# State tiles of the sample recurrences in halves, with each half's load queued behind an earlier half's store

## The chip, the cores and the metric

The kernel runs on one core of one Trainium2 chip. The metric is the device time of one execution in microseconds (us), as a median over runs. Below, TensorE is PE (its weight loads PEld), VectorE DVE, ScalarE ACT, GpSimd POOL; SP is SyncE, which here only issues DMAs, one after the other.

## What is computed

One step of a hybrid decoder layer for a prompt (512 tokens) and for 8 samples of 8 tokens each, which share the weights. The change is in the two recurrences of the samples. Each sample carries a state from HBM into the step and back to HBM:

```python
# SSD: h (16 heads, 64, 128 states) per sample
y_inter = jnp.einsum('btgn,bgjpn->btgjp', cc, h) * jnp.exp(cum)[..., None]
h_new = h * jnp.exp(cum[:, -1])[..., None, None] + jnp.einsum('bsgj,bsgjp,bsgn->bgjpn', to_end, xc, bc)
# mLSTM: c (4 heads, 128, 256) per sample, with n as a 257th column
num = jnp.einsum('btsh,bshv->bthv', s, vc) + s_inter[..., None] * jnp.einsum('bthd,bhdv->bthv', qc, c_st)
c_new = scale[..., None, None] * c_st + jnp.einsum('bsh,bshd,bshv->bhdv', w_end, kc, vc)
```

So every state is read once by a matmul that gives a part of the output, is scaled, has a product added, and is stored. The outputs include both new states of all 8 samples in float32.

## The kernel before

One program does the whole layer. Its long part is the projections: `gemm` (L201 to L203) and the token-major `gemm_tok` (L772 to L774, and L764 and L765 for the samples) multiply weights of [128, 128] blocks with activations of 256 or 320 columns; each product takes three matmuls, since weights and activations are split into a high and a low half. `split_w` loads a weight unit of 512 KB into `raw` on SP's queue (L176), casts it on ACT (L181, `whi`), subtracts on DVE (L188, `wlo`) or, for the other half of the columns, on ACT and by an adding DMA from POOL (L185, L186). `raw` has two buffers, `whi` and `wlo` three each.

The order of the instructions of each engine in this part of the program is set before the run, by a scheduler that estimates the times of the whole program. Each engine then works through its list in order: an instruction whose data is not there holds up everything behind it on the same engine. That holds for PE's matmuls and for SP's DMAs. The recurrences are not a phase of their own: the scheduler mixes them into the projections, the SSD part into the stretch from about 110 to 220 us, the mLSTM part into that from about 265 to 390 us.

**SSD samples** (L651 to L737). The pool `ssds` has a tag `t4` of three buffers of [128, 1024] float32. `xdts` and `xes` (inputs of the recurrence, made at L661 and L667) are the first two tiles in it, and the states `h0` the next eight, one for each sample. The profile calls an `h0` tile `h`. A loop of four steps (`b`) takes two samples at a time (`hb`): two loads of 512 KB (L711), then four matmuls `ps_hs` (L715), one for each pair of group `g` and sample `hb`. Each of these has only 32 output rows and writes its own quarter of the PSUM tile's partitions, `q = 32 * (2 * g + hb)`. Then, for each sample, POOL scales the whole state (L722), two matmuls `ps_hu` give the update (L725), DVE adds them half by half (L726), and one store sends the state out (L728). `stacks` (L637 to L649) prepares the operands of the `ps_hu` matmuls.

**mLSTM samples** (L899 to L937). The pool `mls` has a tag `t4` of three buffers of [128, 4, 258] float32 for the states `c0` (the profile: `c`). Here the samples come one at a time: a load of 516 KB (L909), four matmuls `ps_nh` (L911), one for each head `h`, each with 32 output rows in its own quarter, then four matmuls `ps_cu` (L918), each followed by a DVE instruction that scales and adds (L919), and one store (L921).

A float32 matmul is two matmul instructions in the trace, so four such matmuls are shown there as x8.

A buffer is free for the next load once the store of the state that was in it has landed; SP waits for that at the head of its queue, and what stands behind it there waits too, the weight loads of L176 among them.

Of the kernel before, what the change touches and what calls it, by code (L numbers as in the profile page):

```python
# [1 line left out]

# [9 lines left out]
F32 = mybir.dt.float32  # L12
# [3 lines left out]
ALU = mybir.AluOpType  # L16
# [100 lines left out]
def build(nc, tc, ctx, I, O):  # L117
# [24 lines left out]
    def BP(name="b"):  # L142
        return pb.tile([P, 512], F32, name=name, tag="b")
# [490 lines left out]
    ssd_prompt(1)  # L634


    def stacks(pool, a, b, hb, nb=1):  # L637

        r, o = slice(32 * hb, 32 * hb + 32), slice(32 - 32 * hb, 64 - 32 * hb)
        l = slice(64, 96)  # L640
        sa_ = pool.tile([96, a.shape[-1]], F32R, name="sta", tag="sta", bufs=nb)
        sb_ = pool.tile([96, b.shape[-1]], F32R, name="stb", tag="stb", bufs=nb)
# [12 lines left out]
    xes = sd.tile([TS, 16, 64], F32, name="xes", tag="t4", bufs=3)  # L655
    btk = sd.tile([TS, 2, P], F32, name="btk")
    for g in range(2):
        ps = BP("ps_xts")
        for j in range(4):
            TE.transpose(ps[:TS, j * P:(j + 1) * P], xs[:, g * 4 + j, TP:T], ident)  # L660
        V.tensor_tensor(xdts[:, 8 * g:8 * g + 8, :], ps[:TS, :].rearrange("p (h k) -> p h k", h=8),  # L661
                        CT[:TS, 4, 32 + 8 * g:40 + 8 * g].unsqueeze(2).to_broadcast([TS, 8, 64]), op=ALU.mult)
# [16 lines left out]
    for g in range(2):  # L679
        psb = BP("ps_ls")  # L680
        pb3 = psb.rearrange("p (h t) -> p h t", h=8)
        for h in range(8):
            mm(psb[:, h * TS:(h + 1) * TS], sel[:80, 8 * g + h:8 * g + h + 1].to_broadcast([80, P]), cumst[:, TP:T],
               start=h == 0, stop=h == 7, skip_group_check=True)
        A.activation(decs[:, 8 * g:8 * g + 8, :], pb3[:, :, 7:TS:8], AF.Exp)
        lm = sd.tile([TS, 8, TS], F32, name="lms", tag="ts", bufs=1)
        V.tensor_tensor(lm, pb3[:TS], CT[:TS, 4, 8 * g:8 * g + 8].unsqueeze(2).to_broadcast([TS, 8, TS]), op=ALU.subtract)
        G.tensor_tensor(lm, lm, masks8, op=ALU.add)
        A.activation(lm, lm, AF.Exp)
        pcb = BP("ps_cbs")  # L690
        mm(pcb[:TS, :TS], bc[:, g, TP:T], bc[:, 2 + g, TP:T], start=True, stop=True)
        V.tensor_tensor(lm, lm, pcb[:TS, :TS].unsqueeze(1).to_broadcast([TS, 8, TS]), op=ALU.mult)
        for h in range(8):
            k, j = h % 2, (8 * g + h) // 2
            mm(psi[64 * k:64 * k + 64, j * TS:(j + 1) * TS], xdts[:, 8 * g + h, :], lm[:, h, :], start=True, stop=True,
               skip_group_check=True)
    yds = sd.tile([P, 8, TS], F32, name="yds", tag="ts", bufs=1)
    G.tensor_tensor(yds, xs[:, :, TP:T], PAR("dskip").unsqueeze(2).to_broadcast([P, 8, TS]), op=ALU.mult)
# [8 lines left out]
    hbs = [stacks(sd, btk.rearrange("p g k -> p (g k)"), xes.rearrange("p h k -> p (h k)"), hb, 2) for hb in range(2)]  # L707
    for b in range(4):
        hns = [sd.tile([P, 16, 64], F32, name="h0", tag="t4", bufs=3) for _ in range(2)]
        for hb in range(2):  # L710
            S.dma_start(hns[hb], I["h0"][4 * hb + b])  # L711
        for g in range(2):
            for hb in (1, 0):
                q = 32 * (2 * g + hb)
                mm(psh[q:q + 32, :], cpad[:, g, 4 * hb + b, :],  # L715
                   hns[hb][:, 8 * g:8 * g + 8, :].rearrange("p h k -> p (h k)"),
                   start=b == 0, stop=b == 3, skip_group_check=True)
        for hb in range(2):
            bb, hn, (bst, xst) = 4 * hb + b, hns[hb], hbs[hb]
            bm = sd.tile([96, 256], F32R, name="bm", tag="bm", bufs=1)  # L720
            A.activation(bm, bst.bitcast(F32), AF.Copy, scale=C32("bmask")[:96, b:b + 1])
            G.tensor_tensor(hn, hn, decs[:, :, bb:bb + 1].to_broadcast([P, 16, 64]), op=ALU.mult)  # L722
            for g in range(2):
                ps = BP("ps_hu")
                mm(ps, bm[:, g * P:(g + 1) * P], xst[:, g * 512:(g + 1) * 512], start=True, stop=True)  # L725
                V.tensor_tensor(hn[:, 8 * g:8 * g + 8, :], hn[:, 8 * g:8 * g + 8, :],  # L726
                                ps.rearrange("p (h k) -> p h k", h=8), op=ALU.add)
            S.dma_start(O["ssms"][bb], hn.rearrange("p h k -> p (h k)"))  # L728
# [168 lines left out]
    V.tensor_tensor(kws, psk[:TS, :].rearrange("p (h k) -> p h k", h=4),  # L897
                    wendm[:TS, 4, :].unsqueeze(2).to_broadcast([TS, 4, P]), op=ALU.mult)
    for hb in range(2):  # L899
        r = slice(32 * hb, 32 * hb + 32)  # L900
        kst, vst = stacks(ms, kws.rearrange("p h k -> p (h k)"), vts.rearrange("p h k -> p (h k)"), hb)
        psn = BP("ps_nh")
        for h in range(4):
            mm(psn[32 * h:32 * h + 32, 0:257], ds_[r, h, r], vt[4][r, h, 0:257], start=True, stop=False,
               tile_position=(32 * hb, 32 * h), skip_group_check=True)
        for b in range(4):
            bb = 4 * hb + b
            c0 = ms.tile([P, 4, 258], F32, name="c0", tag="t4", bufs=3)
            S.dma_start(c0, I["c0"][bb])  # L909
            for h in range(4):  # L910
                mm(psn[32 * h:32 * h + 32, 0:257], qpad[:, h, bb, :], c0[:, h, 0:257], start=False, stop=b == 3,  # L911
                   skip_group_check=True)
            km = ms.tile([96, 512], F32R, name="km", tag="km", bufs=1)
            A.activation(km, kst.bitcast(F32), AF.Copy, scale=C32("bmask")[:96, b:b + 1])
            cn = c0
            for h in range(4):
                ps = BP("ps_cu")
                mm(ps[:, 0:258], km[:, h * P:(h + 1) * P], vst[:, h * 258:(h + 1) * 258], start=True, stop=True)  # L918
                V.scalar_tensor_tensor(cn[:, h, :], c0[:, h, :], es[:, h, 8 * bb + 7:8 * bb + 8], ps[:, 0:258],  # L919
                                       op0=ALU.mult, op1=ALU.add)  # L920
            S.dma_start(O["cs"][bb], cn)  # L921
# [1490 lines left out]
```

## Time and profile before

| | us |
|---|---|
| time, median of 3 runs (1120.54 to 1121.95) | 1121.05 |
| the profiled execution's own time | 1117.7 |
| its span, first to last instruction | 1115.9 |
| PE busy, share of the span | 1095.6, 98% |
| DVE busy, share | 771.4, 69% |
| ACT busy, share | 609.8, 55% |
| POOL busy, share | 223.5, 20% |
| share of PE in the chain that ended last | 81% |
| DMA queue of SP, share of 16 engines' span | 38.7% |

PE is busy nearly all the time, so a microsecond of work more or less on PE moves the end by about as much, unless it falls into a wait. Where PE's busy time is below the length of a stretch, it waited for something; the view of the waits names what. The profile also gives the clock that PE was granted, as a share of full speed: the mean over the span is 0.996.

### The profile page before, as it was taken

The page shows a single profiled execution, that of the slowest core. Times are in us where ns is not written, and L with a number is a line of the kernel's source. Part 1 is how long each engine was busy: PE and PEld are TensorE (multiplying, and loading weights), DVE is VectorE, ACT ScalarE, POOL GpSimd, SP SyncE. Part 2 cuts the span into 40 slices and gives each one's busy share as a digit, 9 for nine tenths or more (in the row PEclk, how much of TensorE's full clock was granted, in tenths as well). Part 3 has the DMA queues.
Part 4 walks back from the last instruction along what each step waited for, and adds up shares of the span by engine and source line. Part 5 has one row for each costly group of instructions (what it writes and reads, how often), then busy time and mean ns, then how long its engine had stood idle before and what let it go on. Part 6 is the DMA issues. An engine that isn't in the chain of part 4 may idle for free.

```text
span 1115.9 us, 21276 instructions
## 1 busy us (share of the span) xinstructions
PE 1095.6 (98%) x8355; PEld 1043.4 (94%) x8355; DVE 771.4 (69%) x1521; ACT 609.8 (55%) x1130; POOL 223.5 (20%) x309
## 2 busy tenths in 40 slices
PE   9999999899999999999999999999999999999997
PEld 8999889798998999999988889999999999999997
DVE  6796875447786685568745455675578878887655
ACT  6877534246464365566534545644465556556654
POOL 1333544313113021110144401100000210020000
PEclk9999999999999999999999999999999999999999
DMA  6685565536464437973487755742552873397432
GB/s 210 159 165 130 132 180 144 172 71 163 128 204 111 118 101 260 294 279 96 151 268 263 254 204 163 229 158 88 169 157 82 188 170 88 83 234 219 103 138 85
DMA packets 60584, 184.44 MB, mean 165 GB/s; under 512 B 6684, under 2 KB 10908, under 8 KB 59972
## 3 DMA queue, kind: packets, MB, share of 16 engines
q1 hardware_dynamic: 44324, 142.19, 38.7%
q0 software_dynamic: 15872, 40.38, 17.5%
q8 instruction: 65, 1.06, 0.4%
q10 hardware_dynamic: 288, 0.52, 0.1%
q14 instruction: 35, 0.29, 0.1%
HBM read 153.75 MB, written 29.30 MB: 164 GB/s over the span
## 4 chain that ended last, share of the span: by engine, by line
PE 81%; DVE 6%; DMA 6%; ACT 5%; issue 2%; SPq 0%; DVEq 0%; ACTq 0%; POOLq 0%
PE ps_in L201 5%; PE ps_in L203 5%; PE ps_in L202 5%; PE ps_g L1725 3%; PE ps_g L1726 3%; PE ps_g L1727 3%; PE ps_u L1726 2%; PE ps_u L1725 2%; PE ps_u L1727 2%; PE ps_o L201 2%; PE ps_o L203 2%; PE ps_o L202 2%; PE ps_dn L201 2%; PE ps_dn L203 2%; PE ps_dn L1932 2%; PE ps_dn L202 2%
## 5 line engine op out<-in xcount | busy, mean ns | idle before, releaser
L201 PE MATMUL ps_in<-uh,whi 128*128 128x320 f32 (+1 forms) x544 | 165.9, 305 | 0.0
L203 PE MATMUL ps_in<-uh,wlo 128*128 128x320 f32 (+1 forms) x544 | 163.3, 301 | 0.1
L202 PE MATMUL ps_in<-ul,whi 128*128 128x320 f32 (+1 forms) x544 | 162.7, 299 | 0.0
L181 ACT CAST whi<-raw 128x1024 fp32r<-128x1024 f32 (+1 forms) x102 | 102.8, 1011 | 80.6 <-PE ps_in L202 19.5
L188 DVE TENSOR_TENSOR wlo<-raw,whi 128x512 fp32r<-128x512 f32 (+1 forms) x94 | 87.9, 935 | 62.4 <-ACT whi L181 61.8
L201 PEld LDWEIGHTS ps_in<-uh,whi 128*128 128x128 f32 x544 | 103.6, 190 | 2.6 <-issue 1.2
L203 PEld LDWEIGHTS ps_in<-uh,wlo 128*128 128x128 f32 x544 | 103.4, 190 | 2.0 <-issue 1.3
L202 PEld LDWEIGHTS ps_in<-ul,whi 128*128 128x128 f32 x544 | 103.6, 190 | 0.7
L186 POOL DMA_DIRECT2D wlo<-win x32 | 28.3, 886 | 94.5 <-ACT wlo L185 84.0
L1725 PE MATMUL ps_g<-b,whi 128*128 128x288 f32 x144 | 42.7, 297 | 1.2 <-ACT cc L1793 1.0
L1725 PE MATMUL ps_u<-b,whi 128*128 128x288 f32 x144 | 42.8, 298 | 0.0
L1726 PE MATMUL ps_u<-b,whi 128*128 128x288 f32 x144 | 42.5, 295 | 0.0
L1726 PE MATMUL ps_g<-b,whi 128*128 128x288 f32 x144 | 42.5, 295 | 0.0
L201 PE MATMUL ps_xo<-qh,whi 128*128 128x288 f32 x128 | 37.8, 300 | 1.0 <-ACT f_xo L1407 1.0
L201 PE MATMUL ps_o<-mixm_h,whi 128*128 128x256 f32 (+1 forms) x128 | 38.0, 297 | 0.3 <-ACT whi L181 0.3
L201 PE MATMUL ps_xq<-u2h,whi 128*128 128x320 f32 (+1 forms) x128 | 38.2, 303 | 0.0
L774 PE MATMUL ps_v<-wlo,uh 128*128 128x256 f32 x128 | 37.0, 293 | 1.1 <-DMA wlo<-wv 1.1
L202 PE MATMUL ps_xq<-u2l,whi 128*128 128x320 f32 (+1 forms) x128 | 38.0, 298 | 0.0
L203 PE MATMUL ps_xq<-u2h,wlo 128*128 128x320 f32 (+1 forms) x128 | 37.9, 297 | 0.0
L202 PE MATMUL ps_o<-mixm_l,whi 128*128 128x256 f32 (+1 forms) x128 | 37.9, 297 | 0.0
L203 PE MATMUL ps_xo<-qh,wlo 128*128 128x288 f32 x128 | 37.7, 296 | 0.0
L202 PE MATMUL ps_xo<-ql,whi 128*128 128x288 f32 x128 | 37.6, 295 | 0.0
(777 smaller groups left out, 3913.8 us busy)
## 6 DMA issues: line engine op xcount, KB each, us to landing
raw<-win SPq DMA_DIRECT2D x35, 512.0 KB, 3.8
raw<-wout SPq DMA_DIRECT2D x17, 512.0 KB, 4.2
kva<-kc SPq DMA_DIRECT2D x16, 512.0 KB, 6.5
kva<-vc SPq DMA_DIRECT2D x16, 512.0 KB, 6.4
raw<-wxq SPq DMA_DIRECT2D x13, 512.0 KB, 3.8
raw<-wgate SPq DMA_DIRECT2D x13, 512.0 KB, 5.3
raw<-wup SPq DMA_DIRECT2D x13, 512.0 KB, 3.5
wlo<-win POOLq DMA_DIRECT2D x24, 256.0 KB, 5.6
```

Source lines behind the costliest of these rows:

```text
L181: A.copy(hi[:, :n], raw[:, :n])
L186: G.dma_start(lo[:, a:b], src[:, a:b], accum_op=ALU.add)
L188: e.tensor_tensor(lo[:, a:b], raw[:, a:b], hi[:, a:b].bitcast(F32), op=ALU.subtract)
L201: mm(ps, wh, ah, start=i == 0, stop=False)
L202: mm(ps, wh, al, start=False, stop=False)
L203: m = mm(ps, wl, ah, start=False, stop=i == len(tiles) - 1)
L774: m = mm(o, ah, lo[:, j:j + 256], start=False, stop=k == KT - 1, skip_group_check=True)
L1725: mm(ps, wh, b[0][:, k, :], start=start and k == 0, stop=False, skip_group_check=True)
L1726: mm(ps, wh, b[1][:, k, :], start=False, stop=False, skip_group_check=True)
L1727: m = mm(ps, wl, b[0][:, k, :], start=False, stop=k == 3, skip_group_check=True)
L1932: mm(ps, wh, bl, start=False, stop=False, skip_group_check=True)
```

## The change

The states are held in halves. In the SSD part the tag has six buffers of [128, 512] in place of three of [128, 1024]; `xdts` and `xes` become two halves each, one for each group. In the mLSTM part it has six of [128, 2, 258], each with two heads. Each half has its own load, its own POOL scaling (SSD), and its own store. A list `keep` collects the stores in order, and `tc.issue_after` puts a load behind a certain store in SP's queue: that of the half four places back. The matmuls of a half stand right behind its load in the code, so that the SSD loop now goes over `hb` and then `g`, where it went over `g` and then `hb` after both loads. `stacks` takes its second operand in parts.

```diff
+    def behind(ins):
+        return tc.issue_after(ins.ins) if ins is not None else nullcontext()
+
     def stacks(pool, a, b, hb, nb=1):
...
-        A.copy(sb_[r, :], b[r, :])
-        V.tensor_tensor(sb_[o, :], b[r, :], sb_[r, :].bitcast(F32), op=ALU.subtract)
-        A.copy(sb_[l, :], b[r, :])
+        for k, part in enumerate(b):
+            c = slice(k * w, (k + 1) * w)
+            A.copy(sb_[r, c], part[r, :])
+            V.tensor_tensor(sb_[o, c], part[r, :], sb_[r, c].bitcast(F32), op=ALU.subtract)
+            A.copy(sb_[l, c], part[r, :])
...
-    xdts = sd.tile([TS, 16, 64], F32, name="xdts", tag="t4", bufs=3)
-    xes = sd.tile([TS, 16, 64], F32, name="xes", tag="t4", bufs=3)
+    xdts, xes = [[sd.tile([TS, 8, 64], F32, name=k, tag="half", bufs=6) for _ in range(2)] for k in ("xdts", "xes")]
...
-    G.tensor_tensor(xes, xdts, wend[:TS, 4, :].unsqueeze(2).to_broadcast([TS, 16, 64]), op=ALU.mult)
+    for g in range(2):
+        G.tensor_tensor(xes[g], xdts[g], wend[:TS, 4, 8 * g:8 * g + 8].unsqueeze(2).to_broadcast([TS, 8, 64]), op=ALU.mult)
...
+    keep = []
     for b in range(4):
-        hns = [sd.tile([P, 16, 64], F32, name="h0", tag="t4", bufs=3) for _ in range(2)]
+        hns, kept = {}, list(keep)
         for hb in range(2):
-            S.dma_start(hns[hb], I["h0"][4 * hb + b])
-        for g in range(2):
-            for hb in (1, 0):
+            for g in range(2):
+                hns[hb, g] = hn = sd.tile([P, 8, 64], F32, name="h0", tag="half", bufs=6)
+                with behind(kept[-4 + 2 * hb + g] if b else None):
+                    S.dma_start(hn, I["h0"][4 * hb + b][:, 8 * g:8 * g + 8, :])
                 q = 32 * (2 * g + hb)
-                mm(psh[q:q + 32, :], cpad[:, g, 4 * hb + b, :],
-                   hns[hb][:, 8 * g:8 * g + 8, :].rearrange("p h k -> p (h k)"),
+                mm(psh[q:q + 32, :], cpad[:, g, 4 * hb + b, :], hn.rearrange("p h k -> p (h k)"),
                    start=b == 0, stop=b == 3, skip_group_check=True)
...
-            G.tensor_tensor(hn, hn, decs[:, :, bb:bb + 1].to_broadcast([P, 16, 64]), op=ALU.mult)
             for g in range(2):
+                hn = hns[hb, g]
+                G.tensor_tensor(hn, hn, decs[:, 8 * g:8 * g + 8, bb:bb + 1].to_broadcast([P, 8, 64]), op=ALU.mult)
                 ps = BP("ps_hu")
                 mm(ps, bm[:, g * P:(g + 1) * P], xst[:, g * 512:(g + 1) * 512], start=True, stop=True)
-                V.tensor_tensor(hn[:, 8 * g:8 * g + 8, :], hn[:, 8 * g:8 * g + 8, :],
-                                ps.rearrange("p (h k) -> p h k", h=8), op=ALU.add)
-            S.dma_start(O["ssms"][bb], hn.rearrange("p h k -> p (h k)"))
+                V.tensor_tensor(hn, hn, ps.rearrange("p (h k) -> p h k", h=8), op=ALU.add)
+                keep.append(S.dma_start(O["ssms"][bb][:, g * 512:(g + 1) * 512], hn.rearrange("p h k -> p (h k)")))
...
-            c0 = ms.tile([P, 4, 258], F32, name="c0", tag="t4", bufs=3)
-            S.dma_start(c0, I["c0"][bb])
+            c0, kept = [], list(keep)
+            for p in range(2):
+                c0.append(ms.tile([P, 2, 258], F32, name="c0", tag="half", bufs=6))
+                with behind(kept[-4 + p] if len(kept) > 3 else None):
+                    S.dma_start(c0[p], I["c0"][bb][:, 2 * p:2 * p + 2, :])
             for h in range(4):
-                mm(psn[32 * h:32 * h + 32, 0:257], qpad[:, h, bb, :], c0[:, h, 0:257], start=False, stop=b == 3,
+                mm(psn[32 * h:32 * h + 32, 0:257], qpad[:, h, bb, :], c0[h // 2][:, h % 2, 0:257], start=False, stop=b == 3,
...
+                if h % 2:
+                    keep.append(S.dma_start(O["cs"][bb][:, h - 1:h + 1, :], c0[h // 2]))
```

Since the scheduler sets the order, the diff does not show where the instructions come to stand. On SP, at the end of the SSD samples, before the change (`h_1924` to `h_1981` are whole states, `raw` a weight unit):

```order
L728 DMA o_ssms<-h_1925 128x1024
L711 DMA h_1980<-h 128x1024
L176 DMA raw<-wv 128x1024 x2
L728 DMA o_ssms<-h_1952 128x1024
L711 DMA h_1981<-h 128x1024
L728 DMA o_ssms<-h_1953 128x1024
```

The same place on SP after the change (`h_1977` to `h_2022` are half states, the last eight of the sixteen among them):

```order
L735 DMA o_ssms<-h_1977 128x512
L721 DMA h_2013<-h 128x512
L735 DMA o_ssms<-h_1980 128x512
L721 DMA h_2016<-h 128x512
L735 DMA o_ssms<-h_1983 128x512
L721 DMA h_2019<-h 128x512
L176 DMA raw<-wv 128x1024
L735 DMA o_ssms<-h_1986 128x512
L721 DMA h_2022<-h 128x512
```

Stores and loads now alternate, and a load stands behind a store two halves later than the one that frees its buffer: `h_2022` takes the buffer of `h_1980`, and stands behind the store of `h_1986`; before, `h_1981` took the buffer of `h_1952` and stood right behind that store.

On PE, where the last round of `ps_hs` stands, before the change:

```order
L773 MATMUL ps_v<-whi,ul 128x256
L715 MATMUL ps_hs<-h_1981,cpad 32x512
L715 MATMUL ps_hs<-h_1980,cpad 32x512
L715 MATMUL ps_hs<-h_1981,cpad 32x512
L715 MATMUL ps_hs<-h_1980,cpad 32x512
L774 MATMUL ps_v<-wlo,uh 128x256
```

After the change the matmuls of the four halves of this round stand apart; this is the first of them, between an update matmul and the projection:

```order
L581 MATMUL ps_xt<-c_75,xs 128x128 x4
L733 MATMUL ps_hu<-stb,bm 128x512
L723 MATMUL ps_hs<-h_2013,cpad 32x512
L781 MATMUL ps_v<-wlo,uh 128x256
L779 MATMUL ps_v<-whi,uh 128x256
L780 MATMUL ps_v<-whi,ul 128x256
```

In the whole program the sixteen `ps_hs` matmuls stood in four runs of four; now the first four stand together and the other twelve each alone, with matmuls of the full 128 output rows on both sides.

On PE, where the second half of the mLSTM samples begins, before the change (`c_3563` to `c_3605` are whole states; L904 also writes quarters of `ps_nh`):

```order
L904 MATMUL ps_nh<-vts,ds__3394 32x257 x4
L911 MATMUL ps_nh<-c_3563,qpad 32x257 x4
L911 MATMUL ps_nh<-c_3584,qpad 32x257 x4
L911 MATMUL ps_nh<-c_3605,qpad 32x257 x4
L846 MATMUL ps_n<-vt_2442,dm 128x257
```

and after it (`c_3616` to `c_3642` are halves with two heads each):

```order
L912 MATMUL ps_nh<-vts,ds__3435 32x257 x4
L922 MATMUL ps_nh<-c_3616,qpad 32x257 x2
L922 MATMUL ps_nh<-c_3618,qpad 32x257 x2
L858 MATMUL ps_c<-vt_2483,kw 128x257
L922 MATMUL ps_nh<-c_3640,qpad 32x257 x2
L855 MATMUL ps_n<-cst__3267,qs 128x257
L853 MATMUL ps_n<-vt_2483,dm 128x257
L922 MATMUL ps_nh<-c_3642,qpad 32x257 x2
```

The 32 `ps_nh` matmuls of L911 stood in 7 runs without a full-width matmul in them; they now stand in 13, ten of which have only the two heads of one half. The number of matmuls on PE is the same in both programs, and so is PE's order from the output projection (`ps_o1`) on.

More of the change, by code (lines that the diff above doesn't have):

```diff
@@ L1 @@
-from contextlib import ExitStack
+from contextlib import ExitStack, nullcontext
 import ml_dtypes
@@ L640, in stacks @@
         l = slice(64, 96)
+        w = b[0].shape[-1]
         sa_ = pool.tile([96, a.shape[-1]], F32R, name="sta", tag="sta", bufs=nb)
-        sb_ = pool.tile([96, b.shape[-1]], F32R, name="stb", tag="stb", bufs=nb)
+        sb_ = pool.tile([96, w * len(b)], F32R, name="stb", tag="stb", bufs=nb)
         A.copy(sa_[r, :], a[r, :])
@@ L660, in build @@
             TE.transpose(ps[:TS, j * P:(j + 1) * P], xs[:, g * 4 + j, TP:T], ident)
-        V.tensor_tensor(xdts[:, 8 * g:8 * g + 8, :], ps[:TS, :].rearrange("p (h k) -> p h k", h=8),
+        V.tensor_tensor(xdts[g], ps[:TS, :].rearrange("p (h k) -> p h k", h=8),
                         CT[:TS, 4, 32 + 8 * g:40 + 8 * g].unsqueeze(2).to_broadcast([TS, 8, 64]), op=ALU.mult)
@@ L694, in build @@
             k, j = h % 2, (8 * g + h) // 2
-            mm(psi[64 * k:64 * k + 64, j * TS:(j + 1) * TS], xdts[:, 8 * g + h, :], lm[:, h, :], start=True, stop=True,
+            mm(psi[64 * k:64 * k + 64, j * TS:(j + 1) * TS], xdts[g][:, h, :], lm[:, h, :], start=True, stop=True,
                skip_group_check=True)
@@ L706, in build @@
     psh = BP("ps_hs")
-    hbs = [stacks(sd, btk.rearrange("p g k -> p (g k)"), xes.rearrange("p h k -> p (h k)"), hb, 2) for hb in range(2)]
+    hbs = [stacks(sd, btk.rearrange("p g k -> p (g k)"), [t.rearrange("p h k -> p (h k)") for t in xes], hb, 2) for hb in range(2)]
+    keep = []
     for b in range(4):
-        hns = [sd.tile([P, 16, 64], F32, name="h0", tag="t4", bufs=3) for _ in range(2)]
+        hns, kept = {}, list(keep)
         for hb in range(2):
-            S.dma_start(hns[hb], I["h0"][4 * hb + b])
-        for g in range(2):
-            for hb in (1, 0):
+            for g in range(2):
+                hns[hb, g] = hn = sd.tile([P, 8, 64], F32, name="h0", tag="half", bufs=6)
+                with behind(kept[-4 + 2 * hb + g] if b else None):
+                    S.dma_start(hn, I["h0"][4 * hb + b][:, 8 * g:8 * g + 8, :])
@@ L898, in build @@
                     wendm[:TS, 4, :].unsqueeze(2).to_broadcast([TS, 4, P]), op=ALU.mult)
+    keep = []
     for hb in range(2):
         r = slice(32 * hb, 32 * hb + 32)
-        kst, vst = stacks(ms, kws.rearrange("p h k -> p (h k)"), vts.rearrange("p h k -> p (h k)"), hb)
+        kst, vst = stacks(ms, kws.rearrange("p h k -> p (h k)"), [vts.rearrange("p h k -> p (h k)")], hb)
         psn = BP("ps_nh")
```

8 lines of the change are left out of this document (3 added, 5 removed).

## The prediction

> **What bounds the kernel now.** I read the page first, for the busy share of each engine.
>
> ```profile
> span 1115.9 us, 21276 instructions
> PE 1095.6 (98%) x8355; PEld 1043.4 (94%) x8355; DVE 771.4 (69%) x1521; ACT 609.8 (55%) x1130; POOL 223.5 (20%) x309
> ```
>
> PE works for 1095.6 of 1115.9 us. So the end moves with what is added to PE's work and with what is taken from its idle 20.3 us; the other engines matter only where PE waits for them. The view of the waits on PE therefore comes next, then the same view for SP's queue.
>
> ```profile
> PE ps_hs L715 <- DMA h<-h: 2.6, 1, 2.6
> PE ps_nh L911 <- DMA c<-c: 1.9, 1, 1.9
> ...
> PE ps_v L774 <- DMA wlo<-wv: 1.1, 2, 0.9
> ```
>
> Columns: what waited and for what, us in total, number of waits, the longest. PE's two longest waits are for state loads, each a single one, and a third, shorter one for weights stands in the same part of the program. Everything that the change touches lies in two stretches; the view by windows gives them (window, length, busy time and instructions of PE, PEld, DVE, ACT, POOL; granted clock; DMA share; GB/s).
>
> ```profile
> 140.00:220.00 80.00, 76.53 (x593) 66.33 (x592) 45.36 (x91) 27.89 (x48) 33.91 (x27) 0.98 0.56 159
> 270.00:390.00 120.00, 118.12 (x855) 108.95 (x854) 88.35 (x242) 59.02 (x133) 22.15 (x26) 0.99 0.50 136
> ...
> 205.00:206.00 1.00, 0.95 (x8) 0.20 (x8) 0.00 (x0) 0.00 (x0) 0.00 (x0) 0.50 0.54 217
> ...
> 208.00:209.00 1.00, 1.00 (x9) 1.00 (x9) 0.00 (x0) 0.33 (x1) 1.00 (x2) 0.84 0.00 0
> 362.00:363.00 1.00, 1.00 (x9) 0.19 (x9) 1.00 (x1) 0.00 (x0) 0.69 (x1) 0.50 0.94 307
> ...
> 365.00:366.00 1.00, 1.00 (x9) 1.00 (x8) 1.00 (x4) 0.48 (x3) 0.00 (x0) 0.83 0.28 51
> ```
>
> PE is idle for 3.47 us in the first stretch and 1.88 us in the second: 5.35 us is all that can be gained there by ending waits. The last four rows show a second price of the two long waits: behind each of them PE ran three windows of 1 us at a granted clock of 0.50 and one at 0.84 or 0.83, which is 3 x 0.5 + 0.16 = about 1.6 us lost after each, 3.2 in both. The timeline shows where the waits came from, on PE and then on SP.
>
> ```profile
> 205.05 1.93 PE L715 MATMUL ps_hs<-h,cpad 128*32 128x512 f32 x8 [2.60 <-DMA h<-h]
> 361.93 1.08 PE L911 MATMUL ps_nh<-c,qpad 128*32 128x257 f32 x8 [1.88 <-DMA c<-c]
> 191.37 0.34 SPq L728 DMA_DIRECT2D o_ssms<-h  x1
> 200.98 0.33 SPq L711 DMA_DIRECT2D h<-h  x1
> 352.95 0.34 SPq L921 DMA_DIRECT2D o_cs<-c  x1
> 358.32 0.34 SPq L909 DMA_DIRECT2D c<-c  x1
> ```
>
> The last state load of the SSD part went out only at 200.98, since SP stood behind the store of 191.37 until it had landed; the load's data came at 205.05. The mLSTM load of 358.32 likewise followed the store of 352.95. So in both places a store must land and a load must land, one after the other, before PE can go on.
>
> **What the change removes.** Behind the change a half is loaded into the buffer of the half six back, and stands in the queue behind the store of the half four back. When SP reaches it, the store that it really waits for was issued two stores earlier. The store's landing is thus mostly off the chain, and what is left is the DVE addition, a store's issue, a load's issue and its landing.
>
> ```profile
> L726 DVE TENSOR_TENSOR h<-h,ps_hu x16: 675/680/689, 146.7 to 215.8; 128x512 f32<-128x512 f32 x16
> h<-h SPq DMA_DIRECT2D x8, 512.0 KB, 4.0
> raw<-wdown SPq DMA_DIRECT2D x8, 256.0 KB, 3.7
> ```
>
> That is 0.68 + 0.34 + 0.33 + 3.7 to 4.0, about 5.2 us, where no row shows a half state; 3.7 is the nearest row of that size, and a half saves hardly anything against a whole. Between a half's update and the matmul that needs the load behind its store, PE has matmuls that take, at their durations in this trace, an estimated 7 to 9 us, at the tightest place (the first half of the third round) some 6. I estimate that both long waits go, with their slow clock behind them: 2.60 + 1.88 + 3.2 = **7.7 us**. The wait for `wlo` (0.9) I take as gone too, since PE comes to that place several microseconds later (below) and SP no longer stands for 9.6 us. Bounds: all idle time and the clock loss, 5.35 + 3.2 = 8.6 us, and nothing, if the half loads are waited for in place of the whole ones. I take 7.7 + 0.9 = 8.6, nearest to the waits' own rows.
>
> **What the change adds on PE.** The number of matmuls is the same, but `ps_hs` and `ps_nh` matmuls have 32 output rows, and the trace shows that such neighbours run at the same time.
>
> ```profile
> 141.35 0.28 PE L201 MATMUL ps_in<-uh,whi 128*128 128x256 f32 x1
> 141.47 0.28 PE L202 MATMUL ps_in<-ul,whi 128*128 128x256 f32 x1
> 141.68 1.07 PE L715 MATMUL ps_hs<-h,cpad 128*32 128x512 f32 x8
> 142.68 0.33 PE L617 MATMUL ps_yi<-lm,xdt 128*64 128x128 f32 x2
> ...
> 190.38 1.02 PE L589 MATMUL ps_h<-xe,btok 128*128 128x512 f32 x2
> 191.23 0.60 PE L581 MATMUL ps_xt<-c,xs 128*128 128x128 f32 x4
> ...
> 271.53 0.59 PE L846 MATMUL ps_n<-vt,dm 128*128 128x257 f32 x2
> 271.96 0.60 PE L851 MATMUL ps_c<-vt,kw 128*128 128x257 f32 x2
> ...
> 300.54 0.63 PE L911 MATMUL ps_nh<-c,qpad 128*32 128x257 f32 x6
> 301.11 0.38 PE L918 MATMUL ps_cu<-stb,km 96*128 96x258 f32 x1
> 301.42 0.62 PE L911 MATMUL ps_nh<-c,qpad 128*32 128x257 f32 x2
> 301.97 0.38 PE L201 MATMUL ps_in<-uh,whi 128*128 128x256 f32 x1
> 302.19 0.28 PE L202 MATMUL ps_in<-ul,whi 128*128 128x256 f32 x1
> ```
>
> Read these by the distance from start to start, since ends are modelled. One full-width float32 matmul of 512 columns (x2) takes 191.23 - 190.38 = 0.85 us, one of 257 columns 0.43 us. Four `ps_hs` (x8) together take 1.00 us, hardly more than one. Three `ps_nh` (x6) take 0.57 us, and a single one (x2) still takes 0.55. So the time goes by rounds, one round being up to four neighbours, and a lone matmul costs a whole round. A run of them has edges too: inside it 0.12 to 0.15 beyond the rounds (0.55 - 0.43, 1.00 - 0.85), take 0.13; ahead of it the full-width matmul takes longer than the 0.12 from 141.35 to 141.47 (0.21 ahead of `ps_hs`, and the 258 columns of `ps_cu` 0.31 ahead of `ps_nh`), 0.09 to 0.19 more, take 0.15; behind it 0.22 for L201 in place of 0.12, 0.10 more. An edge is thus about 0.38 us a run.
>
> `ps_hs`: four runs of one round before; after it one run of four matmuls and twelve lone ones, 13 runs and 13 rounds. Added: 9 x (0.85 + 0.38) = 11.1 us. `ps_nh`: 7 runs with 10 rounds before (a run of up to four matmuls is one round, the longest has three); 13 runs with 14 rounds after. Added: 4 x 0.43 + 6 x 0.38 = 4.0 us. Together **15.1 us**. Bounds: without the edges 9 x 0.85 + 4 x 0.43 = 9.4; with the larger entry of 0.19 everywhere 15 x 0.04 = 0.6 more, 15.7. I take 15.1, since the lone `ps_nh` at 301.42 is the very thing that is multiplied. No part of it lies beside other PE work: each lone matmul has full-width matmuls on both sides. It can vanish only into idle time, and that is already counted as gained.
>
> A rule bears on the edges. The Trainium skill, TensorEngine Tiling (Array Packing), Tiling Modes, Key Properties, says that "Mode switching requires drain", and that tiles work independently; by it each of the 15 added runs pays an entry and an exit, as 0.55 against 0.43 in the trace agrees; without such a drain the sum below would be 9.4 - 8.6 = +0.8 us in place of +6.5.
>
> **What else is added.** SP issues 16 more loads and 16 more stores at 0.33 to 0.34 us, 10.9 us spread over some 170 us in which it mostly waits; the weight loads behind them come later by one or two issues, and the bound on that is the weight wait that exists now, 0 to 0.9 us. POOL scales in halves.
>
> ```profile
> L722 POOL TENSOR_TENSOR h<-h,decs x8: 1920/1936/2383, 142.9 to 209.0; 128x1024 f32<-128x1024 f32 x8
> L587 POOL TENSOR_TENSOR xe<-xdt,wend x8: 1034/1045/1688, 110.0 to 212.2; 128x512 f32<-128x512 f32 x8
> ```
>
> Eight instructions of 1.94 us become sixteen; L587 has the size of a half and takes 1.05, so POOL gains 16 x 1.05 - 8 x 1.94 = 1.3 us of work in a stretch where it is busy for 33.91 of 80 us. The split copies of `stacks` on ACT likewise lie beside PE (ACT is busy for 27.89 of 80 us). I cost both at nothing; if the cover went, the 1.3 us and some tenths would come in.
>
> **The sum.** +15.1 - 7.7 - 0.9 = **+6.5 us**, on the profiled execution's own time 1117.7 us: 1124.2. That execution lies 3.35 us below the median of the three runs (its span another 1.8 below it), so the median comes to 1121.05 + 6.5 = **1127.6 us**.
>
> **Rivals.**
> A, *no change*: the edges of lone runs cost little, because the weight load and the entry of the next matmul overlap, so that 9.4 us stand against 8.6: +0.8, 1121.9. For it: the entry ahead of `ps_hs` is only 0.09 at 141.47. Against: the 0.55 at 301.42.
> B, *faster*: a lone matmul of 32 rows runs partly beside its full-width neighbours, so that a lone `ps_hs` costs half a round. Then 9 x 0.43 + 4 x 0.43 = 5.6 against 8.6: -3.0, 1118.1. It decides from the point where the added work is below 8.6 - 2.2 = 6.4 us, about 0.5 us for each of the 13 added rounds. For it: no row shows a lone `ps_hs`. Against: the lone `ps_nh` costs its full round of 0.43 and more.
> C, *the change does not do what it says*: the half loads still come late, at one of the two places or at a tight one in the third round. Such a wait keeps 2.6 us and 1.6 of clock: +6.5 + 4.2 = +10.7, 1131.8; with no wait gone at all, +15.1, 1136.2. For it: these rows.
>
> ```profile
> SPq L711 <- DMA o_ssms<-h: 18.8, 5, 9.2
> ...
> o_ssmp<-hs SPq DMA_DIRECT2D x2, 256.0 KB, 5.5
> ```
>
> A store's landing held SP's state loads five times, once for 9.2 us, and a store of 256 KB took 5.5 us, no less than the whole state's. Against it: two more places of slack, and PE itself comes later by the added work.
> A rule speaks for C: the Trainium skill, DMA: Bandwidth & Descriptors, Anatomy of one DMA, gives about 2.0 us for each transfer whatever its size, beside bytes at 436 GB/s (an estimate from it: 3.2 us for a whole state, 2.6 for a half), and Rules for kernel authors wants transfers of 1 MiB and more; 4.0 and 3.7 in the trace agree that a half is hardly sooner. By that rule the sixteen extra pairs would price at C's +10.7 if they reached PE, and at +6.5 if they stay hidden.
>
> **How the numbers follow.** About 0.2%, 2.2 us here, is what a measurement of this kernel can tell from no change. The forecast (added work about as summed, waits gone) has a chance of 0.62, with its own range 1124.5 to 1130; A 0.17; B 0.08; C 0.13. Low end 1120.5: it takes in A and leaves out most of B. High end 1134.5: it takes in C with one wait and the upper edge (1131.8 + 0.6) with some of a second wait, and leaves out C's worst. Faster 0.08 (B), within 0.2% 0.17 (A), slower 0.75 (forecast and C).
>
> **What would show it.** Right: `ps_hs` and `ps_nh` no longer wait for a DMA; the granted clock stays near 1.00 between 200 and 220 and between 360 and 380 us; twelve `ps_hs` groups of x2, each about 1 us from start to start; PE's busy time up by more than 10 us while its idle time falls. Wrong: lone `ps_hs` of half a microsecond (B), lone runs without edges (A), waits of PE for half loads or for weights behind them (C). The forecast would fail altogether if PE's matmuls were regrouped by something that the order does not show, or if work after 435 us, where PE's order is the same, moved.

## The result, and the profile after

The changed kernel takes 1136.1 us (median of 6 runs, 1135.15 to 1139.15), against 1121.1 us for the kernel before (6 runs, 1115.74 to 1122.73): 1.0141 times as long, 95% interval 1.0117 to 1.0165. That is 15 us slower where 6.5 us were forecast, and outside the range of the prediction (its high end was 1134.5). The profiled execution was the longest of the six, 1139.15 us by its own time; that of before was 1117.7, so the two traces lie 21.5 us apart, some 6 us more than the medians.

The page of the changed kernel begins:

```profile
span 1137.4 us, 21362 instructions
PE 1112.4 (98%) x8355; PEld 1047.3 (92%) x8355; DVE 769.3 (68%) x1523; ACT 611.2 (54%) x1134; POOL 226.3 (20%) x318
```

The number of PE instructions is the same, and they take 16.8 us more. PE's idle time did not fall: 1137.4 - 1112.4 = 25.0 us against 20.3. The waits on PE show what came in place of the ones that went:

```profile
PE ps_o L201 <- ACT mixs_h L192: 4.1, 1, 4.1
PE ps_o L201 <- ACT whi L181: 3.8, 2, 2.4
...
PE ps_ss L1472 <- DVE ssqxo L1548: 1.0, 1, 1.0
...
PE ps_o L202 <- DVE mixs_l L193: 0.9, 1, 0.9
...
PE ps_nh L922 <- DMA c<-c: 0.3, 1, 0.3
```

The wait of `ps_hs` for a state is gone, that of `ps_nh` is 0.3 us in place of 1.9. But the output projection `ps_o`, which waited for 0.3 us in all before (for `whi`), now waits for its activations `mixs_h` and later for its weights `whi`. The windows tell the same by stage (columns as in the prediction):

```profile
140.00:220.00 80.00, 80.00 (x557) 62.49 (x556) 39.94 (x80) 24.38 (x42) 33.06 (x33) 1.00 0.56 152
...
270.00:390.00 120.00, 119.66 (x852) 107.28 (x851) 86.61 (x238) 61.94 (x134) 27.22 (x36) 1.00 0.51 138
390.00:440.00 50.00, 45.05 (x317) 44.22 (x316) 39.24 (x83) 28.86 (x55) 9.59 (x14) 0.93 0.45 149
```

The last stretch before the change:

```profile
390.00:440.00 50.00, 50.00 (x380) 49.85 (x379) 36.62 (x74) 30.82 (x56) 10.36 (x15) 1.00 0.51 175
```

Where the recurrences run, PE is now idle for 0.34 us in all and its clock is full; the loss lies behind them, at 390 to 440 us, where PE was busy for all 50 us before. The timeline of the changed kernel there, first PE, then ACT:

```profile
411.71 0.38 PE L947 MATMUL ps_hts<-c,hns 128*128 128x128 f32 x2
416.15 0.74 PE L201 MATMUL ps_o<-mixs_h,whi 128*128 128x256 f32 x3 [4.06 <-ACT mixs_h L192]
417.77 0.58 PE L202 MATMUL ps_o<-mixs_l,whi 128*128 128x256 f32 x1 [0.89 <-DVE mixs_l L193]
...
411.76 1.04 ACT L181 CAST whi<-raw 128x1024 fp32r<-128x1024 f32 x1 [2.44 <-PE ps_in L202]
412.71 2.56 ACT L1017 ACTIVATE mixm_h<-qk,ghalf 128x512 fp32r<-128x512 f32 x4
415.18 0.34 ACT L948 COPY qk<-ps_hts 128x256 f32<-128x256 f32 x1
415.43 4.68 ACT L192 CAST mixs_h<-xs 128x576 fp32r<-128x576 f32 x8
```

And before the change, again first PE, then ACT:

```profile
400.60 0.38 PE L936 MATMUL ps_hts<-c,hns 128*128 128x128 f32 x2
...
405.62 0.31 PE L203 MATMUL ps_in<-uh,wlo 128*128 128x320 f32 x1
405.77 0.28 PE L201 MATMUL ps_o<-mixs_h,whi 128*128 128x256 f32 x1
...
401.02 0.37 ACT L937 COPY qk<-ps_hts 128x256 f32<-128x256 f32 x1
401.29 4.70 ACT L192 CAST mixs_h<-xs 128x576 fp32r<-128x576 f32 x8
405.88 0.42 ACT L992 ACTIVATE tmp<-tmp 128x256 f32<-128x256 f32 x1
```

`ps_hts` is the last PE work of the mLSTM samples, and the copy behind it ends them. In both kernels the eight casts of `mixs_h` follow that copy at once. Before, it came at 401.02, 4.8 us ahead of the first `ps_o` at 405.77, and the casts ran beside the last 36 matmuls of `ps_in`, which stood behind `ps_hts` on PE. Now `ps_hts` is the very last instruction of PE ahead of `ps_o`, so the casts fall into PE's idle time, and four `mixm_h` activations (2.56 us) stand between as well.

In the trace of every kernel below the first of these casts starts 0.25 to 0.32 us after that copy, whether the copy comes at 390.32 us or at 415.18: the casts follow the end of the samples. The code says why they may have to: `mixs_h` is the first tile of the pool `big0` (L974 in the changed kernel), which takes the place of the pool `mls` on the same side of the memory when that is closed (L949). Its buffer is free only once the samples' last instructions and stores are through. That this tie, and not only ACT's order, holds the casts is read from the code; no run separates the two.

To the two waits, 4.06 and 0.89 us, comes the clock, which fell behind the first, at 416:

```profile
416.00:417.00 1.00, 0.74 (x3) 0.41 (x3) 1.00 (x4) 1.00 (x3) 0.00 (x0) 0.78 0.90 369
417.00:418.00 1.00, 0.23 (x1) 0.23 (x2) 1.00 (x3) 1.00 (x3) 0.00 (x0) 0.50 0.07 29
...
422.00:423.00 1.00, 1.00 (x6) 1.00 (x6) 0.87 (x3) 0.55 (x2) 1.00 (x4) 0.50 0.00 0
423.00:424.00 1.00, 1.00 (x8) 1.00 (x8) 1.00 (x3) 0.49 (x1) 1.00 (x2) 0.80 0.00 0
```

Six windows at 0.50, in five of which PE worked throughout, and parts of two at 0.8: about 5.2 x 0.5 + 0.4 = 3.0 us. Together 4.06 + 0.89 + 3.0 = about 8.0 us at this one place.

So the loss splits by stage. The table holds starts read from the two traces: of the last `ps_v` ahead of 260 us (L772 before, L779 after), of the first `ps_o` on `mixs_h` (first output product), of the first on `mixm_h` (second output product), of the first `ps_xq` (the projection behind it); and the span:

| us | before | after | later by |
|---|---|---|---|
| last `ps_v`, the SSD samples are through | 250.0 | 255.8 | 5.8 |
| first `ps_o`, `mixs_h` | 405.8 | 416.1 | 10.3, of it 4.06 in the wait |
| first `ps_o`, `mixm_h` | 456.7 | 471.0 | 14.3 |
| first `ps_xq` | 522.2 | 542.1 | 19.9 |
| span | 1115.9 | 1137.4 | 21.5 |

Up to the wait PE is 10.3 - 4.1 = 6.2 us late, close to the 6.5 of the prediction. The next 8 us are the late `mixs_h`. Then 5.6 us are lost in the second output product, where PE waited twice for weights (3.8 us), with a granted clock of 0.50 for 3 us behind that and 0.84 in the next (about 1.7 us more):

```profile
499.55 0.41 PE L201 MATMUL ps_o<-mixm_h,whi 128*128 128x320 f32 x1 [2.36 <-ACT whi L181]
...
501.56 0.41 PE L201 MATMUL ps_o<-mixm_h,whi 128*128 128x320 f32 x1 [1.46 <-ACT whi L181]
```

### The profile page after: what moved, and what is told of

Same layout as the page of the kernel before. It is cut to its first block, busy times and chain, and to the rows that moved or that the text cites. A ratio compares the mean times of both kernels' runs of the same rounds, so it can differ in the third digit from the quotient of the medians.

```text
span 1137.4 us, 21362 instructions
## 1 busy us (share of the span) xinstructions
PE 1112.4 (98%) x8355; PEld 1047.3 (92%) x8355; DVE 769.3 (68%) x1523; ACT 611.2 (54%) x1134; POOL 226.3 (20%) x318
## 4 chain that ended last, share of the span: by engine, by line
PE 80%; DVE 7%; DMA 7%; ACT 4%; issue 2%; SPq 0%; POOL 0%; DVEq 0%; ACTq 0%; POOLq 0%
PE ps_in L201 5%; PE ps_in L202 5%; PE ps_in L203 4%; PE ps_g L1736 3%; PE ps_g L1737 3%; PE ps_g L1738 3%; PE ps_u L1737 2%; PE ps_u L1736 2%; PE ps_u L1738 2%; PE ps_o L203 2%; PE ps_o L202 2%; PE ps_o L201 2%; PE ps_v L781 2%; PE ps_dn L201 2%; PE ps_dn L203 2%; PE ps_dn L1943 2%
## 5 line engine op out<-in xcount | busy, mean ns | idle before, releaser
L201 PE MATMUL ps_o<-mixs_h,whi 128*128 128x256 f32 (+1 forms) x128 | 39.0, 307 | 4.1 <-ACT mixs_h L192 4.1
L202 PE MATMUL ps_o<-mixs_l,whi 128*128 128x256 f32 (+1 forms) x128 | 38.9, 305 | 0.9 <-DVE mixs_l L193 0.9
L203 PE MATMUL ps_o<-mixs_h,wlo 128*128 128x256 f32 (+1 forms) x128 | 38.6, 302 | 0.0
L203 PE MATMUL ps_o<-mixm_h,wlo 128*128 128x256 f32 (+1 forms) x128 | 38.4, 304 | 0.2 <-DVE wlo L188 0.2
```

The source lines that it names most:

```text
L201: mm(ps, wh, ah, start=i == 0, stop=False)
L202: mm(ps, wh, al, start=False, stop=False)
L203: m = mm(ps, wl, ah, start=False, stop=i == len(tiles) - 1)
```

## The experiments

The theory after the result: two prices, independent of each other. **One** is PE's, the lone matmuls, as predicted. **The other** is the order behind the store four places back: it leaves four halves in flight where six buffers (three whole states before) allow six, so each half comes later, the mLSTM samples end only with the input projection, and `mixs_h` is late. The rivals: the 32 more DMAs as such make weights late; ACT's order alone (the `mixm_h` activations) is at fault; or the late casts merely follow from PE's later position. The first four ran on one chip (the kernel before: 1121.9 us there), the next four on another (1119.5), the last two on a third (1119.5).

**Only ACT's order.** The activations of `mixm_h` stand behind the casts of `mixs_h`; all else as in the changed kernel.

```diff
-            split(mixs_h[:, j, :], mixs_l[:, j, :], y[:, j, :])
+            mixs.append(A.copy(mixs_h[:, j, :], y[:, j, :]))
+            V.tensor_tensor(mixs_l[:, j, :], y[:, j, :], mixs_h[:, j, :].bitcast(F32), op=ALU.subtract)
...
-        A.activation(mixm_h[:, j, 0:TP], hm, AF.Copy, scale=ghalf[:, j:j + 1])
+        with tc.issue_after(mixs[-1].ins):
+            A.activation(mixm_h[:, j, 0:TP], hm, AF.Copy, scale=ghalf[:, j:j + 1])
```

> Only ACT's order at the end of the input projection is changed: the eight casts of mixs_h stand ahead of the mixm_h activations. Theory (late end of the mLSTM samples: mixs_h takes the memory of their pool, so its casts wait for the samples' last instructions and stores, and the output projection waits for the casts): the four mixm_h activations took 2.56 us ahead of the last copy and the casts, so the wait of the output projection falls from 4.06 to about 1.5 us, and 2.5 to 5 us are gained on the changed kernel (1136.1): 1131 to 1133.5. Rival (the output projection is late because the weights come late behind the 32 extra DMAs): nothing gained, 1135 to 1137, the wait moves to the weights.

Measured: 1127.9 us (7 runs), 1.0067 times before, interval 1.0041 to 1.0093. Its waits on PE:

```profile
PE ps_o L201 <- ACT whi L181: 3.8, 2, 2.5
PE ps_o L201 <- ACT mixs_h L992: 1.6, 1, 1.6
```

The wait for `mixs_h` is 1.6 us, as expected, so it is these casts that PE waits for, and their place in ACT's order is a part of the loss, not the whole of it. But the median is only 6.0 us above the kernel before in the same set, where the changed kernel is 15.1 above it in its own: a gain of 9 us, more than the 2.5 to 5 expected, while the profiled execution (1135.7) came down little. The same kernel again:

> The first experiment once more, since its median (1127.9) lay 7.8 us below its profiled execution, and 8 us below the changed kernel, where 2.5 to 5 us were expected. Theory (the casts of mixs_h and what stands behind them on ACT also hold the weight casts of the output projection, so that its weights lose their lead and PE waits for them near 500 us): 1126 to 1131 again, and a profiled execution near that median has a stage from the second output product to the next projection of 66 to 69 us in place of 71 to 73. Rival (the median of the first set was chance): 1131 to 1134.

Measured: 1129.1 us (6 runs), 1.0083 [1.0055, 1.0111], 9.6 us above the kernel before: the gain is real, and by this set 5 to 6 us. In this second profiled execution (1129.75 us) the stage from the second output product to `ps_xq` took 65.2 us (66 to 69 were expected), in the first 72.7, in the changed kernel 71.1, and 65.5 in the kernel before. PE's wait for weights near 500 us thus comes in some executions of the same kernel and not in others. That the late casts make it more frequent fits the medians, but was not shown.

**The queue order left out.** Halves as they are, but no load is put behind a store.

```diff
     def behind(ins):
-        return tc.issue_after(ins.ins) if ins is not None else nullcontext()
+        return nullcontext()
```

> Halves as in the changed kernel, but no load is queued behind a store by hand; a load waits only for its buffer, six halves back. Theory (the order behind the store four back leaves only four halves in flight, which stretches the mLSTM samples up to the end of the input projection): the samples end earlier, mixs_h is cast ahead of need, and the output projection does not wait: 8 us gained on the changed kernel at that place. ps_hs still has 12 runs (12 rounds), ps_nh 8 runs, so PE's work stays 9 to 10 us above before; with both long waits gone 1121 to 1124, with one or two half loads waited for 1125 to 1129. Rival (the extra DMAs as such make the weights late): 1133 to 1137, with the wait at the output projection as in the changed kernel.

Measured: 1126.8 us (12 runs), 1.0033 [1.0015, 1.0051]. PE does not wait for `mixs_h` at all; one half load is waited for, 1.6 us. The last update matmul of the mLSTM samples shows that they end earlier; here are its groups, before, after, and in this kernel (the last number is the start of the last one):

```profile
L918 PE MATMUL ps_cu<-stb,km x32: 282/284/472, 278.2 to 386.9; 96*128 96x258 f32 x32
...
L929 PE MATMUL ps_cu<-stb,km x32: 280/284/473, 284.5 to 403.4; 96*128 96x258 f32 x32
...
L929 PE MATMUL ps_cu<-stb,km x32: 279/284/474, 283.5 to 387.6; 96*128 96x258 f32 x32
```

403.4 in the changed kernel, 387.6 without the order, with the same halves, the same 32 extra DMAs and a start only 1.0 us apart. So the extra DMAs are not the cause of the late end, and the order is. Against before, leaving it out takes 15.1 - 4.9 = about 10 us off. Some 3 of these are PE's own work: without the order there are fewer lone runs (12 of `ps_hs` and 8 of `ps_nh`, in place of 13 each), and PE reaches the first `ps_o` at 408.9 where in the changed kernel it stood ready at 416.15 - 4.06 = 412.1.

**One half of the change each.** The SSD samples as changed with the mLSTM samples as before, and the reverse (the loop of the other recurrence is that of the other kernel, word for word, and `stacks` takes what it needs).

> SSD samples as in the changed kernel, mLSTM samples as before (whole tiles). Theory: lone ps_hs add 10 to 11 us, the waits of the SSD part that go give back 5.1 us, the mLSTM wait (1.9 us and its clock) may stay in both; the samples' end is a little later than before, so the output projection waits 0 to 2 us: +5 to +8, 1126 to 1129. Rival (16 of the 32 extra DMA pairs, so half of the 8 us at the output projection and more): 1131 or above.

> SSD samples as before (whole tiles), mLSTM samples as in the changed kernel. Theory: ps_nh adds 4.0 us, the wait that goes gives 1.9 and 1.6 back, so PE alone gives +0.5; the late mixs_h casts stand as in the changed kernel, a wait of 4 to 5 us with about 3.4 us of clock behind it: +8 to +9, 1129 to 1130.5. Rival (lone matmuls are the whole loss and the wait at the output projection follows from PE's later position): +0.5 to +2, 1121.5 to 1123.

Measured: SSD alone 1126.1 us (9 runs), 1.0052 [1.0028, 1.0076]; mLSTM alone 1129.65 us (6 runs), 1.0063 [1.0039, 1.0088]. Both lie where the theory put them, and with the SSD part alone PE waits for `mixs_h` for only 0.6 us. The waits of mLSTM alone:

```profile
PE ps_o L201 <- ACT mixs_h L192: 4.1, 1, 4.1
PE ps_o L201 <- ACT whi L181: 2.1, 2, 1.2
PE ps_v L777 <- DMA wlo<-wv: 1.7, 3, 0.7
```

The full wait for `mixs_h` stands here although PE reaches the first `ps_o` at 407.9, 8 us earlier than in the changed kernel. So the wait does not come from PE's later position; it comes with the mLSTM part.

**The changed kernel again**, for a second profile.

> The changed kernel once more, on the chip of the next three, for a second profile. Both theories: 1134 to 1138. Theory (late casts of mixs_h): the wait of the output projection for mixs_h stands again at about 4 us with a slow clock behind it, since it follows from the order of the instructions; the later wait for weights (3.8 us near 500 us in the first profile) may come or not, and where it is small the execution is 4 to 6 us shorter than 1139.

Measured: 1135.3 us (5 runs), 1.0146 [1.0114, 1.0178]. The wait for `mixs_h` is again 4.1 us, that for weights 3.1. This profiled execution (1135.45 us) lies near the median, and the five rows of the table above come out in it as later by 5.9, 10.1, 13.5, 18.1 and 17.8 us than in the trace of before: the weights near 500 us are late in it too.

**Matmuls together, with and without the order.** In both kernels the four `ps_hs` of a round, and the four `ps_nh` of a sample, stand together: the one on the half that is loaded last comes first, the others behind it. The second kernel also leaves out the queue order of the loads.

```diff
+        first = None
+        for hb, g in ((1, 1), (1, 0), (0, 1), (0, 0)):
+            q = 32 * (2 * g + hb)
+            with behind(first):
+                m_ = mm(psh[q:q + 32, :], cpad[:, g, 4 * hb + b, :], hns[hb, g].rearrange("p h k -> p (h k)"),
+                        start=b == 0, stop=b == 3, skip_group_check=True)
+            first = first or m_
...
+            first = None
+            for h in (3, 2, 1, 0):
+                with behind(first):
+                    m_ = mm(psn[32 * h:32 * h + 32, 0:257], qpad[:, h, bb, :], c0[h // 2][:, h % 2, 0:257], start=False, stop=b == 3,
```

> The changed kernel with its loads queued behind stores as they are, but the four ps_hs of a round and the four ps_nh of a sample stand together (the matmul on the half loaded last comes first, the other three behind it). Theory: the added 15 us of PE work go; the samples end later still (eight mixm_h activations now stand ahead of the last copy and of the mixs_h casts), so the output projection waits 5 to 9 us for mixs_h with 3 us of slow clock behind it: 1120 to 1127. Rival (lone matmuls are the whole loss, the late casts only follow from PE's later position): 1112 to 1117.

> Halves, no load queued behind a store by hand, the matmuls of a round and of a sample together. Theory: PE's work as before (ps_hs 4 runs, ps_nh 7), mixs_h cast ahead of need as in the experiment without the order behind stores, at most one half load waited for: 1115 to 1121, and against that experiment (1126.8) 8 to 10 us less PE work between 140 and 260 us, which is the price of the lone ps_hs. Rival (the 32 extra DMAs cost time by themselves): 1123 to 1128.

Measured: with the order 1131.1 us (6 runs), 1.0106 [1.0079, 1.0132]; without it 1118.1 us (12 runs), 0.9988 [0.9969, 1.0007]. The first missed its expected range (1120 to 1127) on the slow side, and its trace shows how far the samples are behind: PE now waits for their own chain.

```profile
411.70 0.69 PE L954 MATMUL ps_hts<-c,hns 128*128 128x128 f32 x2 [9.73 <-DVE hns L951]
413.46 1.06 PE L201 MATMUL ps_o<-mixs_h,whi 128*128 128x256 f32 x3 [1.08 <-ACT mixs_h L192]
```

9.73 us and 1.08 us: with the lone matmuls taken out PE comes earlier, but the samples do not end earlier. Their last `hns` starts on DVE at 411.29, in the changed kernel at 410.08, although their last `ps_cu` starts 4.5 us sooner; so the gain turns into idle time. PE also waits for `wlo` in the SSD part here, 3.4 us. That rules out the rival by which lone matmuls were the whole loss. In the kernel without the order the samples' last `ps_cu` starts at 376.0, and what PE waits for is small and spread:

```profile
PE ps_o L201 <- ACT whi L181: 2.0, 1, 2.0
PE ps_nh L928 <- DMA c<-c: 1.8, 2, 1.0
PE ps_hs L726 <- DMA h<-h: 1.3, 1, 1.3
```

**Halves for the SSD samples alone**, together and without the order.

> As the one before, but only the SSD samples are in halves; the mLSTM samples as before the change. Theory: the SSD wait of 2.6 us and its slow clock may go, all else as before: 1117 to 1122. Rival (extra DMAs): 1122 to 1125.

Measured: 1118.3 us (12 runs), 0.9993 [0.9973, 1.0012], so no different from before either; its trace still has a wait of 2.0 us for a half state.

**Five places back** in place of four, with the matmuls together; six is what the six buffers ask for by themselves.

> Halves with the matmuls together, each load queued behind the store of the half five places back, between four (1131.1 in the earlier experiment) and six, which is what the buffers ask for by themselves (1118.1). Theory (the order behind the store sets how many halves are in flight, and so how late the mLSTM samples end; ps_cu ends near PE's row 2608 here, 2667 with four, 2524 with none): 1120 to 1127, and the wait at the end of the input projection lies between 0 and the 10.8 us of four places. Rival (any order by hand behind a store costs the same, through what stands behind it on SP): 1129 to 1132.

Measured: 1125.0 us (8 runs), 1.0052 [1.0034, 1.0071]. Four, five and none thus give +11.5, +5.5 and -1.4 us against before, each in its own set. The last `ps_cu` (the last number of each line) starts at 398.9, 390.5 and 376.0:

```profile
L936 PE MATMUL ps_cu<-stb,km x32: 280/285/472, 276.8 to 398.9; 96*128 96x258 f32 x32
...
L936 PE MATMUL ps_cu<-stb,km x32: 279/285/472, 274.4 to 390.5; 96*128 96x258 f32 x32
...
L936 PE MATMUL ps_cu<-stb,km x32: 280/284/470, 275.0 to 376.0; 96*128 96x258 f32 x32
```

The waits at the end of the input projection are 10.8 us, 5.2 (4.2 for `mixs_h` and 1.0 for `mixs_l`), and none. So the loss goes with the number of places; a hand-made order as such does not cost a fixed amount.

The times in one table, as the median minus that of before in the same set:

| us | loads behind the store four back | not ordered |
|---|---|---|
| lone matmuls | +15.1, +15.7 (the change) | +4.9 |
| matmuls together | +11.5 | -1.4 |

Lone matmuls thus cost 6.3 us without the order and some 4 with it; the difference lies within the intervals. No version beats the kernel before beyond its interval.

## Why the prediction was wrong

**PE's added work: right.** A lone `ps_hs` in the trace of the changed kernel:

```profile
151.41 0.28 PE L203 MATMUL ps_in<-uh,wlo 128*128 128x256 f32 x1
151.62 1.05 PE L723 MATMUL ps_hs<-h,cpad 128*32 128x512 f32 x2
152.60 0.38 PE L201 MATMUL ps_in<-uh,whi 128*128 128x256 f32 x1
152.82 0.28 PE L202 MATMUL ps_in<-ul,whi 128*128 128x256 f32 x1
```

From start to start 0.98 us, with 0.21 ahead and 0.22 behind in place of 0.12 each: 1.17 us by itself, where 1.23 was taken. The Trainium skill, TensorEngine Tiling (Array Packing), Tiling Modes, Key Properties, has it that a change of mode drains the engine; 0.09 and 0.10 at the two edges agree with that, as far as this trace shows it. The kernels without the order confirm the sum: with lone matmuls (first line) the last `ps_v` ahead of 260 us starts at 256.3, with the matmuls together at 246.8, 9.5 us for 8 rounds more.

```profile
L779 PE MATMUL ps_v<-whi,uh x128: 278/283/471, 173.3 to 256.3; 128*128 128x256 f32 x128
...
L783 PE MATMUL ps_v<-whi,uh x128: 277/283/386, 167.5 to 246.8; 128*128 128x256 f32 x128
```

Rivals A (free edges) and B (half a round hidden) are out.

**The waits that go: right in this trace, but not a fixed credit.** `ps_hs` no longer waits, `ps_nh` for 0.3 us, and the clock is 1.00 in both stretches. However, the waits of before do not come in every execution: with the SSD part of before, and PE's order in it, unchanged (mLSTM alone) `ps_hs` waited 0.5 us, not 2.6, and the last `ps_v` came at 247.5, not 250.0. Up to the output projection the forecast of +6.5 stands against 6.2 in the traces (SSD part: 11.1 - 4.2 - 0.9 = 6.0 forecast, 5.8 measured).

**The step that failed** is in the part on what the change removes, and with it in the sum. There the order behind the store four places back counts as slack alone ("The store's landing is thus mostly off the chain"), and the half loads are judged only by whether PE would wait at `ps_hs` and `ps_nh`. At those two places the reading holds. But the sum has no term for when the mLSTM samples end: with four halves in flight in place of six their last `ps_cu` starts at 403.4 in place of 386.9, and the wait comes where they are over. In place of nothing the runs showed 8.0 us at the first `ps_o` (4.06 and 0.89 of waiting, 3.0 of slow clock); That 6.5 + 8.0 = 14.5 comes so close to the measured 15 is in part luck: both profiles of the changed kernel also lose time near 500 us (5.6 and 4.6 us), and the trace of before lies 3.4 us under its median. Leaving the order out takes off 10 us with lone matmuls (3 of them PE's work) and 13 with the matmuls together. PE's order, which is set before the run, already shows it: the last `ps_hts` stands behind the last `ps_in`, where 36 matmuls of `ps_in` stood behind it before. The prediction also took PE's order from 435 us on, which is the same, for the same time; the loss lies just ahead of that point and shortly behind it, in the same order of instructions.

**Rival C** ("the half loads still come late") gives 1136.2 with no wait gone, and the measured time is 1136.1. That is a coincidence: its mechanism, PE waiting for half loads, happened for 0.3 us only. The half loads did come late, but what they delayed was the end of the samples.

**The rule on transfer size** (the Trainium skill, DMA: Bandwidth & Descriptors, Rules for kernel authors), which spoke for C, did not decide: with 32 extra transfers of half the size and no order among them the time is that of before (-1.4 us). The fixed 2.0 us that the prediction took from the same page is measured there on transfers that GpSimd issues, and these are SP's. That a half is hardly sooner than a whole holds for the `h` loads of the changed kernel: 4.1 us from issue to landing at the median for a half, 4.0 for a whole before; for `c` it is 3.9 against 4.9.

**What a microsecond on PE is worth.** The prediction took it as about one. The lone matmuls' 9.5 us at 250 us were still 9.4 at the first `ps_o` (408.9 against 399.5), but 3.8 at the first `ps_xq` (527.1 against 523.3) and 6.3 in the medians. PE that comes earlier to the output projection waits there for weights (`whi` 2.0 us, above). So in the kernels that come early some of a gain is given back, in these two profiles more than half.

What stays open: why the weights near 500 us are late in some executions only, which may hold several of the 15 us; and the tie of `mixs_h` to the memory of the samples' pool, which is read from the code and from the order on ACT. Giving `mixs_h` a place of its own was not tried.

## What to carry to other kernels

In these kernels matmuls with a quarter of the output rows cost by rounds of neighbours, not by number: if a finer load granularity splits such a round, count the rounds and the edges. Queueing a load behind the store k places back caps what is in flight at k, whatever the number of buffers; choose k no smaller than the buffers themselves enforce. When a side chain is slowed but nobody waits inside it, ask when it ends, and what can start only then (here, by the code, what takes over its memory): the wait comes there.

## What the runs showed of the hardware

The same pause may or may not bring PE's clock down. In the two executions of the kernel with only ACT's order changed, PE stood for the same 1.61 us ahead of `ps_o`, and for 0.76 and 0.77 us shortly behind. The granted clock (the third number from the end) at 417 us, in the first execution and in the second:

```profile
417.00:418.00 1.00, 1.00 (x10) 1.00 (x9) 1.00 (x3) 1.00 (x3) 0.00 (x0) 1.00 0.88 360
```

```profile
417.00:418.00 1.00, 1.00 (x6) 1.00 (x5) 1.00 (x3) 1.00 (x3) 0.00 (x0) 0.50 0.74 303
```

The second execution ran three such windows at 0.50, as long as behind the 2.6 us of the kernel before. The Trainium skill, TensorE: Matmul & The Clock Gate, What's actually happening, has the clock judged by free-running windows of about 3.4 us. That the same pause has two outcomes agrees with windows that do not start with the pause. If the windows are that long, the pauses of 1.6 and 0.8 us, with work between them, leave none wholly idle, and in the second execution the clock fell all the same.
